# Moving four modulations out of the norms of a two-block transformer kernel

## The chip, the cores and the metric

The kernel runs on one core of a Trainium2 chip. Its time is in device microseconds. The engines are TensorE (PE), VectorE (DVE), ScalarE (ACT), GpSimd (POOL) and SyncE (SP, which issues the DMAs here). All of them run at once; each takes its own instructions in order.

## The reference

256 tokens of width 1,024 pass through two layers of a first block and then two layers of a second block, all in fp32. The change concerns the first block alone:

```python
c_act = jax.nn.silu(c)
for l in range(DEPTH):                                   # 2
    mod = c_act @ w_ada[l] + b_ada[l]
    sh1, sc1, g1, sh2, sc2, g2 = jnp.split(mod, 6, axis=-1)
    h = rmsnorm(x, norm_mix_g[l]) * (1.0 + sc1) + sh1
    z = h @ w_in[l]                                      # four mixers: swa, mla, nsa, moba
    x = x + g1 * (concat(mixers(z)) @ w_out[l])
    h = rmsnorm(x, norm_mlp_g[l]) * (1.0 + sc2) + sh2
    x = x + g2 * (square(relu(h @ w_up[l])) @ w_down[l])
x = rmsnorm(x, final_norm_g)
```

`mod` is six vectors of 1,024 for each layer, one row of `c_act` against a 1,024 x 6,144 matrix. In this text (l, s) is modulation s of layer l: s = 0 is sh1, 1 sc1, 2 g1, 3 sh2, 4 sc2 and 5 g2. Each needs 4 MB of `w_ada`.

## The kernel before

Tokens stand along the free axis and features on the 128 partitions, so x is a tile of 8 chunks of 128 x 256. A weight matrix product is done as three products of fp32r parts: each weight piece of 128 x 1,024 is copied to a high part `wh` on ScalarE (line 299) and its rest `wl` is subtracted on VectorE (line 301); activations are split likewise (`ah`, `al`). One `gemm` is 256 output features: 48 products of 128 x 128 against 128 x 256.

All weights pass through one list in the order of use, `e.stream(...)` (lines 513 to 535). `next_w` (line 304) takes the next piece, splits up to four pieces ahead (NS) and fetches up to eight more (NW); the fetches are one queue on SP. Modulation weights and the compression weights are used whole, without a split.

The program is a list of small steps: `e.add(tag, fn)` appends one, `e.need(tag)` runs steps until none with that tag is left, `e.fill(n)` runs n of them. A planner then orders each engine's instructions by priority and by its own estimate of when their inputs are ready; `high_priority(offset=...)` moves a group forward (200 for the norms, 100 for the splits), and `issue_after(ins)` keeps an instruction behind another one on the same engine.

The stages of the first block are: norm, mixers (line 725), norm, wide products (`w_up` and `w_down` in 16 groups, lines 1066 to 1082), the same again for layer 1, then the last norm. A norm squares x on ScalarE (`square`, line 449), adds the squares on VectorE (`fold`, line 432, `fold_sum`, 441), sums over the partitions on TensorE (`token_sum`, 406, tile `st`), takes the power on GpSimd (`rsqrt`, 401, tile `rsy`), spreads it over the partitions on TensorE (`spread`, 411, tile `bc`), and then scales the 8 chunks: VectorE (603, `nt`), ScalarE (604, `ah`), VectorE (605, `al`).

A modulation is computed in one of two ways. `ada_step` (line 551) takes one of four pairs of weight pieces on TensorE: eight products of 128 x 32 against 128 x 256, which the trace shows as 16 records; four steps are 64 records. `ada_pool` (574) multiplies and adds on GpSimd, one pair at a time, beside the wide products, and `ada_rows` (587) then sums over the partitions with four products on TensorE. Both end in `ada_end` (564): a copy, four small products that turn the row into columns (tile `adat`), and an addition of the bias.

Before, the modulations stand as follows. (0,0) and (0,1) are computed at the start. (0,2), (0,3) and (0,4) are spread over the mixers of layer 0 on TensorE (`ad_early`, `ad_mix`). (1,0), (1,1) and (1,5) are done on GpSimd beside the wide products (`ad_mlp`). (0,5) and (1,4) stand on TensorE in the norm ahead of the wide products of their layer (`ad_norm`, lines 1010 to 1012), and (1,2) and (1,3) in the norm between the layers (`ad_next`, lines 1083 and 997).

Of the kernel before, what the change touches and what calls it, by code (L numbers as in the profile page):

```python
# [13 lines left out]
ALU = mybir.AluOpType  # L14
PSUM = bass.MemoryType.PSUM

P = 128
S = 256
D = 1024
KC = D // P  # L20
DEPTH = 2
# [199 lines left out]
v3 = lambda tl, a: tl.rearrange("p (a b) -> p a b", a=a)  # L221
# [3 lines left out]
class Emit:  # L225
# [157 lines left out]
    def tok_gemm(self, tag, key, act, evac):  # L383
# [14 lines left out]
        for n in range(4):  # L398
            self.add(tag, lambda n=n: piece(n))

    def rsqrt(self, pool, v, cols):
        y = self.t(pool, [P, cols], "rsy", bufs=2)
        self.nc.gpsimd.tensor_tensor(y, v, self.mhalf[:, 0:cols], ALU.pow)  # L403
        return y
# [48 lines left out]

    def rms_wide(self, pool, x, eps):
        box = []
        with self.tc.high_priority(offset=NORM_FIRST):
            for j in range(4):
                self.square(pool, box, flat(x[:, 2 * j : 2 * j + 2, :]))
            return self.rstd(pool, self.fold_sum(box), D, eps)

# [33 lines left out]
def block1(e, ctx, mem0):  # L494
    nc, tc, d = e.nc, e.tc, e.d
    pool = lambda name: ctx.enter_context(tc.tile_pool(name=name, bufs=1))
    cp, zp, ap_ = pool("c1"), pool("z1"), pool("a1")
# [5 lines left out]
    ada = lambda l, s: [("w_ada", l, s, n) for n in range(4)] if l < DEPTH else []  # L503
    zorder = (0, 1, 2, 3, 5, 4, 6, 7, 8)


    ad_early = lambda l: ada(l, 2) if l == 0 else []
    ad_mix = lambda l: ada(l, 3) + ada(l, 4) if l == 0 else []
    ad_norm = lambda l: ada(l,5) if l == 0 else ada(l,4)
    ad_mlp = lambda l: [(1,0),(1,1)] if l == 0 else [(1,5)]  # L510
    ad_next = lambda l: ada(l+1,2)+ada(l+1,3)
    mlp_keys = lambda l: {1 + 6 * i + n: [("w_ada", *p, n)] for i, p in enumerate(ad_mlp(l)) for n in range(4)}
    MEM = 5
    a0 = ada(0, 0) + ada(0, 1)
    start = [[], a0[0:2], a0[2:4], a0[4:6], []]
# [6 lines left out]
    for l in range(DEPTH):  # L522
        W = lambda i: ("w_in1", l, zorder[i])
        ea, am = ad_early(l), ad_mix(l)
        e.stream(*([] if l else [W(0)]), W(1), W(2), *ea[0:2], ("cmp_k1", l), W(3), *ea[2:3], ("cmp_v1", l), W(4), *ea[3:4], W(5))
        e.stream(W(6), *am[0:2], ("w_out1", l, 0), *am[2:3], W(7), ("w_out1", l, 1), *am[3:4], W(8), *am[4:])
        e.stream(("w_out1", l, 2), ("w_out1", l, 3), ("w_up", l, 0), *ad_norm(l))
        nxt = mlp_keys(l)
        for g in range(16):
            if g >= 1:  # L530
                e.stream(("w_up", l, g))
                e.stream(("w_down", l, g - 1))
            e.stream(*nxt.get(g, []))
        e.stream(("w_down", l, 15), *([("w_in1", l + 1, zorder[0])] if l + 1 < DEPTH else []), *ad_next(l))
    e.stream(*MEM_KEYS(0)[MEM:])
# [4 lines left out]
    ca = e.t(cp, [P, KC], "ca")  # L540
# [7 lines left out]

    boxes = {}

# [9 lines left out]
    def blocks(ps, c, w, start, stop):  # L560
        for j in range(4):
            e.mm(ps[32 * j : 32 * j + 32, 0:S], c, w[:, j * S : (j + 1) * S], start, stop)
# [11 lines left out]
    def ada_pool(l, s, n):  # L574
# [4 lines left out]
        for i in range(2):  # L579
# [4 lines left out]
            if not first:  # L584
                nc.gpsimd.tensor_tensor(rows, rows, dst, ALU.add)

    def ada_rows(l, s):
        ps = e.gbank("ada")
        blocks(ps, ones32, boxes[l, s], True, True)
        ada_end(l, s, ps)  # L590

    def ada_add(tag, keys):
        for key in keys:
            e.add(tag, lambda key=key: (ada_pool if tag == "mlp" else ada_step)(*key[1:]))

    def norm_stats(src):
        return e.rms_wide(ap_, src, 1e-6)

# [22 lines left out]
    x = v3(e.unit("x"), KC)  # L621
    nc.sync.dma_start(x, d["xT"])
    e.need("start2")
    bc0 = norm_stats(x)
# [365 lines left out]
    for l in range(DEPTH):  # L990
# [4 lines left out]
        if l:  # L995
            bc0 = norm_stats(x)
            e.need("next")
        norm_apply(x, bc0, A1, mod[:, 0:8], ah, al)
# [10 lines left out]
        ah, al = v3(e.unit("ah", F32R), KC), v3(e.unit("al", F32R), KC)  # L1009
        ada_add("norm", ad_norm(l))  # L1010
        bc0 = norm_stats(x)
        e.need("norm")
        A2 = e.t(ap_, [P, KC], "A2")
# [51 lines left out]

        parts, box, last = {}, [], {}
        steps = mlp_keys(l)
        for g in range(17):
            if l + 1 == DEPTH and g == 1:
                e.add("mlp", late_mem)  # L1070
            if g < 16:
                e.gemm("mlp", [("w_up", l, g)], lambda i: (ah, al), ev_up(g))
            if 1 <= g < 16:
                for c in range(2):
                    e.add("mlp", lambda g=g, c=c: down_piece(g - 1, c))
            if g == 16:
                e.add("mlp", lambda: down_last(15))
            ada_add("mlp", steps.get(g, []))
            for i, p in enumerate(ad_mlp(l)):
                if g == 6 * i + 8:  # L1080
                    e.add("mlp", lambda p=p: ada_rows(*p))
        e.need("mlp")
        ada_add("next", ad_next(l))
        for k in range(KC):
            nc.vector.scalar_tensor_tensor(x[:, k, :], acc[k // 2][:, (k % 2) * S : (k % 2 + 1) * S], mod[:, 40 + k : 41 + k], x[:, k, :], ALU.mult, ALU.add)

    for k in range(MEM, 6):
        mem_gemm(e, 0, k, box[0], mk0, mv0)
    bc = norm_stats(x)
    e.need("mem")  # L1090
# [637 lines left out]
```

## Time and profile before

| | us |
|---|---|
| median of 3 runs (lowest, highest) | 1832.56 (1829.42, 1836.35) |
| the profiled execution's own time | 1832.16 |
| its span, first to last instruction | 1830.3 |
| TensorE busy in the span | 1789.1 |
| VectorE, ScalarE, GpSimd busy | 1333.6, 1016.8, 359.1 |
| moved by DMA | 346.82 MB, 189 GB/s on average |

A product's duration in the profile includes its way through the array, so the next one starts before it has ended: a wide product is listed with 0.28 us, and 40 us hold 339 of them. The granted clock is the share of TensorE's full clock, 2.4 GHz; its other level is half of that. "[1.10 <-POOL rsy]" behind a row says that the engine stood idle for 1.10 us before it and that the instruction which ended the wait was GpSimd's power.

### The profile page before, as it was taken

The numbers are of one execution on the slowest core, as the hardware profiler recorded it, in microseconds if no ns is written. First come the engines' busy times: TensorE is split into PE (matmuls) and PEld (weight loads), VectorE is DVE, ScalarE is ACT, GpSimd is POOL, SyncE is SP. The second block draws the span as 40 slices with busy tenths as digits, with TensorE's granted clock in tenths as the row PEclk, the third lists the DMA queues.
The fourth block names the chain that finished last, engine by engine and source line by source line (L and its number), as shares of the span: only waits on it lengthen the run. The fifth ranks groups of instructions, "written<-read, shape, count | busy, mean of one in ns | idle before, by whom it ended". The sixth has DMA issues, their size and how long they took to land.

```text
span 1830.3 us, 36255 instructions
## 1 busy us (share of the span) xinstructions
PE 1789.1 (98%) x14344; PEld 1674.3 (91%) x14344; DVE 1333.6 (73%) x2209; ACT 1016.8 (56%) x1882; POOL 359.1 (20%) x291
## 2 busy tenths in 40 slices
PE   7999999999998999999999999999999999999998
PEld 6778799987888999998999999999999999999997
DVE  4575775756778655798897997576788797997566
ACT  4444444434555444567777575454556777675552
POOL 0000281800007200002444202200001444202200
PEclk9999999999998999999999999999999999999999
DMA  9873876758348655553444644465554445544451
GB/s 335 308 249 138 310 259 199 256 197 306 115 140 299 226 183 185 165 175 121 162 162 151 202 155 144 168 208 173 194 176 133 148 160 162 184 164 165 154 181 67
DMA packets 98219, 346.82 MB, mean 189 GB/s; under 512 B 12288, under 2 KB 13440, under 8 KB 97792
## 3 DMA queue, kind: packets, MB, share of 16 engines
q1 hardware_dynamic: 98048, 344.50, 55.5%
q8 instruction: 112, 1.84, 0.4%
q14 instruction: 59, 0.48, 0.1%
HBM read 339.01 MB, written 1.05 MB: 186 GB/s over the span
## 4 chain that ended last, share of the span: by engine, by line
PE 89%; DVE 4%; DMA 3%; ACT 3%; issue 1%; SPq 0%; POOLq 0%; DVEq 0%; POOL 0%; ACTq 0%
PE g L337 67%; PE acc L337 10%; PE yps L337 2%; DVE wl L301 1%; ACT wh L299 1%; PE ada L337 1%; PE o L337 1%; PE ds L337 1%; PE sc L337 1%; DMA w<-w_in 1%; PE do L337 1%; DMA w<-w_ada 1%; ACT sb L683 1%; PE xo L337 1%; DMA w<-w_up 1%
## 5 line engine op out<-in xcount | busy, mean ns | idle before, releaser
L301 DVE TENSOR_TENSOR wl<-w,wh 128x1024 fp32r<-128x1024 f32 x518 | 660.8, 1279 | 342.8 <-ACT wh L299 341.1
L299 ACT CAST wh<-w 128x1024 fp32r<-128x1024 f32 x518 | 540.5, 1047 | 494.9 <-PE g L337 328.8
L337 PE MATMUL g<-xh,wh 128*128 128x256 f32 x1664 | 478.2, 288 | 0.3
L337 PE MATMUL g<-xl,wh 128*128 128x256 f32 x1664 | 472.6, 284 | 0.0
L337 PE MATMUL g<-xh,wl 128*128 128x256 f32 x1664 | 471.8, 284 | 0.0
L337 PEld LDWEIGHTS g<-xh,wh 128*128 128x128 f32 x1664 | 319.8, 192 | 12.6 <-issue 6.2
L337 PEld LDWEIGHTS g<-xl,wh 128*128 128x128 f32 x1664 | 319.8, 192 | 0.9 <-issue 0.7
L337 PEld LDWEIGHTS g<-xh,wl 128*128 128x128 f32 x1664 | 319.9, 192 | 0.0
L337 PE MATMUL g<-ah,wh 128*128 128x256 f32 x736 | 211.5, 289 | 5.9 <-ACT ah L604 5.4
L337 PE MATMUL g<-ah,wl 128*128 128x256 f32 x736 | 210.6, 287 | 0.5 <-DVE wl L301 0.5
L337 PE MATMUL g<-al,wh 128*128 128x256 f32 x736 | 210.5, 287 | 0.5 <-DVE al L605 0.5
L403 POOL TENSOR_TENSOR rsy<-rv,mhalf 128x2 f32<-128x2 f32 (+1 forms) x14 | 14.5, 1038 | 936.8 <-DVE rv L420 830.1
L337 PE MATMUL acc<-pt,wh 128*128 128x256 f32 x1024 | 182.9, 280 | 0.0
L1505 POOL PARTITION_BROADCAST E<-rows x64 | 98.0, 1592 | 386.7 <-PE tw L1209 190.9
L1504 ACT ACTIVATE E<-E,ltok 128x128 f32<-128x128 f32 x384 | 124.3, 394 | 60.2 <-POOL E L1505 56.8
L337 PEld LDWEIGHTS acc<-pt,wh 128*128 128x128 f32 x1024 | 156.8, 188 | 0.5 <-issue 0.4
L337 PEld LDWEIGHTS g<-ah,wh 128*128 128x128 f32 x736 | 142.7, 195 | 9.8 <-ACT ah L604 6.4
L337 PEld LDWEIGHTS g<-al,wh 128*128 128x128 f32 x736 | 142.8, 194 | 2.7 <-DVE al L605 1.4
L337 PEld LDWEIGHTS g<-ah,wl 128*128 128x128 f32 x736 | 142.8, 194 | 1.2 <-DVE wl L301 0.7
L337 PE MATMUL acc<-pt,wl 128*128 128x256 f32 x512 | 142.3, 279 | 0.0
L583 POOL TENSOR_SCALAR sb<-w,ca 128x1024 f32<-128x1024 f32 x24 | 90.0, 3751 | 59.9 <-PE ada L337 32.8
L337 PEld LDWEIGHTS acc<-pt,wl 128*128 128x128 f32 x512 | 96.2, 188 | 0.0
(384 smaller groups left out, 3404.8 us busy)
## 6 DMA issues: line engine op xcount, KB each, us to landing
w<-w_ada SPq DMA_DIRECT2D x96, 512.0 KB
w<-w_up SPq DMA_DIRECT2D x64, 512.0 KB
w<-w_down SPq DMA_DIRECT2D x64, 512.0 KB
w<-w_br SPq DMA_DIRECT2D x64, 512.0 KB
w<-w_gl SPq DMA_DIRECT2D x48, 512.0 KB
w<-w_in SPq DMA_DIRECT2D x36, 512.0 KB
w<-w_xs SPq DMA_DIRECT2D x32, 512.0 KB
w<-w_z SPq DMA_DIRECT2D x32, 512.0 KB
```

The costliest lines, as they stand in the source:

```text
L299: nc.scalar.copy(wh, w)
L301: nc.vector.tensor_tensor(wl, w, wh.bitcast(F32), ALU.subtract)
L337: self.last_mm = self.nc.tensor.matmul(o, l, r, start=start, stop=stop)
L403: self.nc.gpsimd.tensor_tensor(y, v, self.mhalf[:, 0:cols], ALU.pow)
L583: nc.gpsimd.tensor_scalar(dst, w, ca[:, 2 * n + i : 2 * n + i + 1], None, ALU.mult)
L683: nc.scalar.activation(self.src(i), self.src(i), AF.Exp, bias=nmx[:, i : i + 1], scale=scale, accum_out=den[:, i : i + 1])
L1504: ex = lambda o, s, r: nc.scalar.activation(o, o, AF.Exp, bias=bias[:, s, r : r + 1])
L1505: nc.gpsimd.partition_broadcast(E, state["rows"][32 * (h % 4) : 32 * (h % 4) + 1, :])
```

## The change

- (0,5) and (1,2) are computed on VectorE beside the wide products of layer 0. `ada_fetch` loads a pair of weight pieces (1 MB) into one of the 11 shared buffers of 128 x 2,048, two groups ahead; `ada_vec` multiplies it by the entries of c and adds, two instructions over 1,024 columns for each pair, ordered behind the last subtraction of the group before (`last["dve"]`). `ada_rows` is put six steps further down the list.
- (1,3) and (1,4) move from the norms into the mixers of layer 1, on TensorE, at the places that (0,2) and (0,3) have in layer 0.
- `ad_norm` and `ad_next` go. In the norms stand products of the identity with itself whose output nobody reads, `warm`: `ahead` of the sums, `between` sums and spread, and `behind` the spread. The numbers are 8, 4, 5 in the norms ahead of the wide products, 12, 4, 5 between the layers, and 0, 5, 5 in the last norm.

```diff
+    def warm(self, o, n):
+        with self.tc.issue_after(self.last_mm.ins):
+            for _ in range(n):
+                self.nc.tensor.matmul(o, self.ident, self.ident, start=True, stop=True)
...
-    def rms_wide(self, pool, x, eps):
+    def rms_wide(self, pool, x, eps, ahead=0, between=0, behind=0):
         box = []
+        if ahead:
+            self.warm(self.gbank("warm")[:, 0:P], ahead)
         with self.tc.high_priority(offset=NORM_FIRST):
             for j in range(4):
                 self.square(pool, box, flat(x[:, 2 * j : 2 * j + 2, :]))
-            return self.rstd(pool, self.fold_sum(box), D, eps)
+            st = self.fold_sum(box)
+            if between:
+                self.warm(self.bank("warm")[:, 0:P], between)
+            bc = self.rstd(pool, st, D, eps)
+            if behind:
+                self.warm(self.bank("warm")[:, 0:P], behind)
+        return bc
...
-    ad_early = lambda l: ada(l, 2) if l == 0 else []
-    ad_mix = lambda l: ada(l, 3) + ada(l, 4) if l == 0 else []
-    ad_norm = lambda l: ada(l,5) if l == 0 else ada(l,4)
-    ad_next = lambda l: ada(l+1,2)+ada(l+1,3)
+    ad_early = lambda l: ada(0, 2) if l == 0 else ada(1, 3)
+    ad_mix = lambda l: ada(0, 3) + ada(0, 4) if l == 0 else ada(1, 4)
+    ad_vec = lambda l: ada(0, 5) + ada(1, 2) if l == 0 else []
...
+    def ada_fetch(l, s, n):
+        boxes["w", l, s, n] = e.unit("adaw")
+        nc.sync.dma_start(boxes["w", l, s, n], d["w_ada"][l, s, n])
+
+    def ada_vec(l, s, n):
+        if n == 0:
+            if "rows" not in boxes:
+                boxes["rows"] = v3(e.unit("rows"), 2)
+            boxes[l, s] = boxes["rows"][:, 0 if l == 0 else 1, :]
+        rows, w = boxes[l, s], v3(boxes.pop(("w", l, s, n)), 2)
+        for i in range(2):
+            c = ca[:, 2 * n + i : 2 * n + i + 1]
+            with tc.issue_after(last["dve"].ins):
+                if n == 0 and i == 0:
+                    nc.vector.tensor_scalar(rows, w[:, i, :], c, None, ALU.mult)
+                else:
+                    nc.vector.scalar_tensor_tensor(rows, w[:, i, :], c, rows, ALU.mult, ALU.add)
+        if n == 3:
+            e.q.insert(min(6, len(e.q)), ("mlp", lambda: ada_rows(l, s)))
...
-            bc0 = norm_stats(x)
-            e.need("next")
+            bc0 = norm_stats(x, 12, 4, 5)
...
-        ada_add("norm", ad_norm(l))
-        bc0 = norm_stats(x)
-        e.need("norm")
+        bc0 = norm_stats(x, 8, 4, 5)
...
+        at = lambda j: 3 + 3 * j // 2
         for g in range(17):
+            for j, key in enumerate(vec):
+                if at(j) == g + 2:
+                    e.add("mlp", lambda key=key: ada_fetch(*key[1:]))
...
+            for j, key in enumerate(vec):
+                if at(j) == g:
+                    e.add("mlp", lambda key=key: ada_vec(*key[1:]))
...
-        ada_add("next", ad_next(l))
...
-    bc = norm_stats(x)
+    bc = norm_stats(x, 0, 5, 5)
```

## Rows read from the trace of the kernel before

**Rows 1.** Stretches: length, busy us per engine (instructions), granted clock, DMA share, GB/s

```profile
67.90:205.40 137.50, 136.18 (x1157) 111.23 (x1155) 87.98 (x267) 60.35 (x149) 2.31 (x2) 1.00 0.63 224
205.40:223.60 18.20, 14.18 (x125) 11.89 (x125) 12.86 (x27) 8.21 (x14) 6.33 (x3) 0.81 0.86 314
423.00:546.20 123.20, 118.80 (x956) 103.30 (x954) 88.39 (x260) 60.87 (x147) 2.57 (x2) 0.99 0.49 169
546.20:565.40 19.20, 14.12 (x125) 12.28 (x125) 13.95 (x26) 8.31 (x14) 8.38 (x4) 0.73 0.90 346
484.00:494.00 10.00, 10.00 (x67) 7.91 (x65) 4.67 (x23) 5.36 (x20) 0.00 (x0) 0.84 0.16 54
757.70:763.70 6.00, 6.00 (x28) 6.00 (x29) 5.17 (x14) 2.75 (x7) 0.00 (x0) 0.50 0.34 98
320.00:360.00 40.00, 40.00 (x339) 40.00 (x338) 29.99 (x22) 19.07 (x22) 38.91 (x13) 1.00 0.77 258
```

**Rows 2.** Timeline of TensorE, layer 0's second norm: start, us, instruction, xcount, [idle <-releaser]

```profile
205.42 3.66 PE L337 MATMUL ada<-w,ca 128*32 128x256 f32 x64
...
210.72 0.71 PE L337 MATMUL bc<-pack,rsy 128*128 128x128 f32 x4 [1.10 <-POOL rsy L403]
...
223.54 0.28 PE L337 MATMUL g<-al,wh 128*128 128x256 f32 x1
```

**Rows 3.** Timeline of VectorE, the same norm

```profile
207.89 0.42 DVE L444 TENSOR_TENSOR fold<-fold 128x256 f32<-128x256 f32 x1
...
211.22 1.23 DVE L301 TENSOR_TENSOR wl<-w,wh 128x1024 fp32r<-128x1024 f32 x1 [1.33 <-ACT wh L299]
...
220.76 1.67 DVE L605 SCALAR_TENSOR_TENSOR al<-nt,mod,ah 128x256 fp32r<-128x256 f32 x2 [0.18 <-ACT ah L604]
```

**Rows 4.** Timeline of TensorE, layer 1's first norm

```profile
409.26 0.61 PE L337 MATMUL st<-ones,fold 128*128 128x1 f32 x4
...
422.87 0.28 PE L337 MATMUL g<-ah,wl 128*128 128x256 f32 x1
...
424.28 0.38 PE L337 MATMUL g<-ah,wl 128*128 128x256 f32 x1 [0.45 <-DVE wl L301]
```

**Rows 5.** Timeline of VectorE, layer 1's first norm

```profile
406.33 0.43 DVE L444 TENSOR_TENSOR fold<-fold 128x256 f32<-128x256 f32 x1
...
411.74 0.87 DVE L603 SCALAR_TENSOR_TENSOR nt<-x,A,bc 128x256 f32<-128x256 f32 x2 [1.61 <-PE bc L337]
...
418.36 0.89 DVE L605 SCALAR_TENSOR_TENSOR al<-nt,mod,ah 128x256 fp32r<-128x256 f32 x2 [0.19 <-ACT ah L604]
```

**Rows 6.** Timeline of VectorE, layer 1's second norm

```profile
548.71 0.43 DVE L444 TENSOR_TENSOR fold<-fold 128x256 f32<-128x256 f32 x1
...
563.78 3.06 DVE L605 SCALAR_TENSOR_TENSOR al<-nt,mod,ah 128x256 fp32r<-128x256 f32 x2 [0.18 <-ACT ah L604]
```

**Rows 7.** Timeline of TensorE, layer 1's second norm: its 48th wide product

```profile
565.35 0.28 PE L337 MATMUL g<-ah,wh 128*128 128x256 f32 x1
```

**Rows 8.** Timeline of TensorE, layer 1's mixers: the longest hole

```profile
482.36 1.08 PE L337 MATMUL o<-pt,z 128*64 128x256 f32 x4 [2.12 <-ACT pt L710]
```

**Rows 9.** Timeline of TensorE, layer 0's wide products: the end of a GpSimd modulation

```profile
384.78 0.64 PE L337 MATMUL ada<-sb,ones 128*32 128x256 f32 x8
...
388.55 0.50 PE L337 MATMUL adat<-pack,pt 128*128 128x4 f32 x4
```

**Rows 10.** Groups by line, 320 to 360 us: busy us, mean ns of one, idle before

```profile
L301 DVE TENSOR_TENSOR wl<-w,wh 128x1024 fp32r<-128x1024 f32 x14 | 24.7, 1769 | 10.1 <-ACT wh L299 10.1
L583 POOL TENSOR_SCALAR sb<-w,ca 128x1024 f32<-128x1024 f32 x6 | 23.3, 3875 | 0.6
L585 POOL TENSOR_TENSOR sb<-sb,sb 128x1024 f32<-128x1024 f32 x7 | 18.2, 2607 | 0.6
```

**Rows 11.** Line 1239, VectorE over 1,024 columns: ns min/median/max

```profile
L1239 DVE SCALAR_TENSOR_TENSOR r<-r,mv,gb x2: 1274/1275/1276, 1819.2 to 1824.3; 128x1024 f32<-128x1024 f32 x2
```

**Rows 12.** Timeline of GpSimd, layer 0's second norm

```profile
217.96 5.92 POOL L583 TENSOR_SCALAR sb<-w,ca 128x1024 f32<-128x1024 f32 x2 [7.30 <-DMA w<-w_ada]
```

More of the change, by code (lines that the diff above doesn't have):

```diff
@@ L504, in block1 @@
     zorder = (0, 1, 2, 3, 5, 4, 6, 7, 8)
-    ad_early = lambda l: ada(l, 2) if l == 0 else []
-    ad_mix = lambda l: ada(l, 3) + ada(l, 4) if l == 0 else []
-    ad_norm = lambda l: ada(l,5) if l == 0 else ada(l,4)
-    ad_mlp = lambda l: [(1,0),(1,1)] if l == 0 else [(1,5)]
-    ad_next = lambda l: ada(l+1,2)+ada(l+1,3)
+    ad_early = lambda l: ada(0, 2) if l == 0 else ada(1, 3)
+    ad_mix = lambda l: ada(0, 3) + ada(0, 4) if l == 0 else ada(1, 4)
+    ad_mlp = lambda l: [(1, 0), (1, 1)] if l == 0 else [(1, 5)]
+    ad_vec = lambda l: ada(0, 5) + ada(1, 2) if l == 0 else []
     mlp_keys = lambda l: {1 + 6 * i + n: [("w_ada", *p, n)] for i, p in enumerate(ad_mlp(l)) for n in range(4)}
@@ L526, in block1 @@
         e.stream(W(6), *am[0:2], ("w_out1", l, 0), *am[2:3], W(7), ("w_out1", l, 1), *am[3:4], W(8), *am[4:])
-        e.stream(("w_out1", l, 2), ("w_out1", l, 3), ("w_up", l, 0), *ad_norm(l))
+        e.stream(("w_out1", l, 2), ("w_out1", l, 3), ("w_up", l, 0))
         nxt = mlp_keys(l)
@@ L533, in block1 @@
             e.stream(*nxt.get(g, []))
-        e.stream(("w_down", l, 15), *([("w_in1", l + 1, zorder[0])] if l + 1 < DEPTH else []), *ad_next(l))
+        e.stream(("w_down", l, 15), *([("w_in1", l + 1, zorder[0])] if l + 1 < DEPTH else []))
     e.stream(*MEM_KEYS(0)[MEM:])
@@ L547, in block1 @@
     mods = [e.t(cp, [P, 48], f"mod{l}") for l in range(DEPTH)]
-    boxes = {}
+    boxes, last = {}, {}
     def ada_step(l, s, n):
@@ L594, in ada_add, with norm_stats @@
             e.add(tag, lambda key=key: (ada_pool if tag == "mlp" else ada_step)(*key[1:]))
-    def norm_stats(src):
-        return e.rms_wide(ap_, src, 1e-6)
+    def norm_stats(src, *idle):
+        return e.rms_wide(ap_, src, 1e-6, *idle)
     def norm_apply(src, bc, A, sh, ah, al):
@@ L1064, in late_mem @@
                 box.append(load_mem(e))
-        parts, box, last = {}, [], {}
+        parts, box, vec = {}, [], ad_vec(l)
+        at = lambda j: 3 + 3 * j // 2
         steps = mlp_keys(l)
```

## The prediction

> **What bounds the kernel now.** I read the stretches first, then the timelines of the norms, and the mixers last. In the wide products TensorE has no idle time (40.00 of 40 us, 0.118 us a product), so a piece of TensorE work put there costs its full length and nothing else in that stage is worth anything [rows 1]. What can be won lies in the four norms between the stages, where TensorE waits for a chain (squares on ScalarE, folds on VectorE, the sums on TensorE, a power on GpSimd, the spread on TensorE, then eight rounds of scaling). I call them A (layer 0, ahead of its wide products), B (layer 1, ahead of its mixers), C (layer 1, ahead of its wide products) and D (the last). Around A and C the mean granted clock is 0.81 and 0.73, and the first 6.0 us of products behind D run at 0.50, that is at 1.2 of 2.4 GHz [rows 1]. In front of the sums the modulation's products stand on TensorE: in A they run from 205.42 to 209.08, while the folds were done at 208.31 [rows 2, 3].
>
> The mixers are full too: 118.80 of 123.20 us in layer 1. Layer 0 has the same products plus three modulations and takes 137.50 us for the same part, from behind the first 48 products to the last product of `w_out1` [rows 1]. This pair of rows prices what the change moves there.
>
> **The norms.** B shows the chain undisturbed from the sums on: sums at 409.26, scaling from 411.74, the last round ended at 419.25 [rows 4, 5], which is 2.48 + 7.51 = 10.0 us; with 0.6 us for the last five of the first 48 products, 10.6 us from the sums to the 48th. In the changed kernel the sums can start 0.06 us behind the last fold.
> - A: folds done 207.89 + 0.42, so 208.37 + 10.6 = 218.9 against 223.54 [rows 2, 3]: 4.6 us. I take 0.8 off since GpSimd lengthens a pair of subtractions there (1.67 against 0.89 us), as it will again, and 0.8 for part of one weight split of 1.23 us that falls into the chain now, at 211.22, and may again [rows 3, 5]. Left: 3.0.
> - B: folds done 406.76, so 417.4 against 422.87: 5.5 us, less 0.4 for a third of a split [rows 3 to 5]. Left: 5.1. The sixteen transfers of 512 KB for two modulations no longer stand ahead of the next weights, whose split is waited for at 424.28 [rows 4].
> - C: folds done 549.14, so 559.8 against 565.35: 5.6 us [rows 6, 7]. GpSimd stretched the last pair by 2.17 us here (3.06 against 0.89), so I take 1.8 off. Left: 3.8.
> - D: no modulation goes. 28 products in 6.0 us at half clock would need 28 x 0.118 = 3.3 us at the full one, 2.7 less [rows 1]; the first of them wait for the scaling anyway, so 2.2, less 0.3 because five idle products ahead of the spread overrun their gap. Left: 1.9.
>
> The idle products: no row shows one. The nearest is the spread, two fp32 products of 128 columns in 0.71 us, 0.36 us each with the tail [rows 2]; from the other side, two records of half the columns of a wide product (0.118 us) make 0.12. I take 0.25, between the two: twelve make 3.0, eight 2.0, four 1.0, five 1.25. In B they start when the accumulation ends at about 403.7 and end at 406.7, before the sums; in A they end at 207.4. Between sums and spread there are 1.1 us free [rows 2]. So they cost nothing on the path; at 0.36 us twelve would hold the sums of B by 1.2 us. That they keep the clock up is judged by B, where TensorE was fed through the norm and no slow stretch follows.
>
> **The mixers of layer 1.** (1,3) and (1,4) go in, at the places that (0,2) and (0,3) have in layer 0. By the two stretches, three modulations cost 137.50 - 123.20 = 14.3 us, 4.8 each, though 64 records in one run take 3.66 and the four turning products 0.50 [rows 1, 2, 9]: split up among other products they take longer than in one run. Two cost 9.5. From it goes what stands at the head of this stretch today, a turning and a wait for a split, 0.50 + 0.45, say 1.0 us [rows 4, 9]. I take +8.5. The upper bound is 9.5 (nothing returned). The lower: 2 x (3.66 + 0.50) = 8.3, less the hole of 2.12 us that they could fill, less the slow clock at 484 to 494 (0.84 over 10 us, so 3.2 us at half rate, 1.6 lost) and less 1.0: +3.6 [rows 1, 8]. Their DMAs, sixteen of 512 KB, enter a stretch whose DMA share is 0.49; with three modulations it is 0.63 in layer 0 [rows 1], so I cost them at nothing.
>
> **The wide products of layer 0.** (0,5) and (1,2) become sixteen VectorE instructions over 1,024 columns at 1.27 us [rows 11], 20.4 us, behind the last subtraction of a group; TensorE gets twice eight products (0.64 us at most) and four turnings (0.50): 2.3 us at most, 1.9 without the tails under which the next product starts [rows 9]. I take +1.9. VectorE is idle in 10.0 of 40 us beside a GpSimd modulation [rows 10], so ten instructions' worth in 46 us has about 11.5 us to go into; what overruns is taken by the three pieces of split weights ahead (24 products each, 2.8 us). The eight fetches of 1 MB add 8.4 MB to 180 us, 47 GB/s on 258, below the 346 GB/s that C shows [rows 1]. Each is issued two groups (some 23 us) ahead of its use. A new instruction waits for its fetch; behind it on VectorE stand the weight splits, and TensorE waits for those. Cost 0 with this cover; without it the price is that of the second rival.
>
> **Sum.** -3.0 - 5.1 - 3.8 - 1.9 + 8.5 + 1.9 = -3.4 us. The profiled execution took 1832.16 us, 1.86 more than its span and 0.40 below the median of the runs. 1832.16 - 3.4 = 1828.8.
>
> **Rivals.**
> - The mixers swallow the two modulations and the norms give all: -4.6 - 5.5 - 5.6 - 2.2 + 3.6 + 1.9 = -12.4, 1819.8 us. For it speaks the hole of 2.12 us right where (0,3) fills the same place in layer 0; against it, that layer 0 is 14.3 us longer with the same fill.
> - VectorE and GpSimd block each other in the wide products. Beside GpSimd's products a split takes 1.77 us on average against 1.23 elsewhere [rows 3, 10]. If each new instruction had to sit out one GpSimd addition (2.61 us), eight of them in the second modulation's 46 us would cost 8 x (1.27 + 2.61) = 31.0 against 11.5 of idle time. The splits run about 6.3 us ahead (three pieces, 8.6, less a copy and a split, 2.3), so TensorE would stand for 31.0 - 11.5 - 6.3 = 13.2 us: 1828.8 + 13.2 = 1842.0, slower than before. It decides from a mean wait of about 1 us per instruction on. Against it: today's mean wait is 0.54 us. The Trainium skill, "SBUF — State Buffer", section "Who interferes with whom", states that a VectorE instruction with two SBUF inputs contends with a GpSimd instruction that reads SBUF, and that the later one fully blocks. By that rule the new instructions are of the kind that blocks, and the sum would be this rival's; the trace shows the blocking, at less than a third of the price.
> - GpSimd starts its first product ahead of the power in A and C. Today it waits until 217.96 for weights that stood behind (0,5) [rows 12]; with these gone they come earlier, and one 3.88 us product [rows 10] in front of the power would delay each of the two norms by up to that: 1828.8 + 2 x 3.9 = 1836.6. Against it: the power has the higher priority when the order is made.
> - The idle products do not hold the clock. The gains by start time stay, those of the clock go: 1.9 in D, about 1 each in A and C: 1832.7.
>
> **How the numbers follow.** Forecast 0.50, with its own range 1824 to 1833; the mixers swallow it 0.22; blocking 0.09; GpSimd first 0.09; clock not held 0.10. The range 1819 to 1838 leaves out the blocking and a little of each tail. 0.5% is 9.2 us, about what a measurement here tells from no change. Faster by more (below 1823): most of the first rival and the forecast's tail, 0.24. Slower by more (above 1841): blocking and a tail, 0.10. Within: 0.66.
>
> **What would show it.** Right: from the folds' end to the 48th product about 11 to 12 us in A, B and C, with a clock near 1 in all four norms; the stretch of layer 1's mixers some 8 us longer, with 128 modulation records in it; the wide products of layer 0 about 2 us longer with no idle TensorE. Wrong: mixers longer by under 5 us (then faster), idle TensorE waiting for a split in 320 to 365 us (then slower), a GpSimd product in front of the power, or a stretch at 0.5 behind a norm.

## The result: slower, and the profile after

The changed kernel takes 1850.24 us (median of 4 runs, 1846.53 to 1851.33) against 1833.82 us (median of 4, 1829.42 to 1836.35): ratio 1.0089, 95% interval [1.0064, 1.0114]. The forecast was 1828.8 with a range to 1838, so it was wrong on the side as well. The profiled execution took 1851.33 us, 19.2 more than that of before; the stages below account for 19.1 of this. Each ends with the start of a product that both traces have: a norm runs from the last product of the stage ahead to the 48th product behind it. The traced execution of held_ad below was a disturbed one (8352 us), so no stage of it is read, and all ratios compare undisturbed executions.

| stage | before, us | after, us | difference | forecast |
|---|---|---|---|---|
| start | 67.90 | 69.61 | +1.7 | 0 |
| mixers, layer 0 | 137.31 | 137.66 | +0.4 | 0 |
| norm A | 18.33 | 22.28 | +3.9 | -3.0 |
| wide products, layer 0 | 180.03 | 181.98 | +1.9 | +1.9 |
| norm B | 19.31 | 16.08 | -3.2 | -5.1 |
| mixers, layer 1 | 123.16 | 135.63 | +12.5 | +8.5 |
| norm C | 19.31 | 17.98 | -1.3 | -3.8 |
| wide products, layer 1 | 178.37 | 180.05 | +1.7 | 0 |
| D and the rest | 1079.00 | 1080.55 | +1.5 | -1.9 |
| sum | | | +19.1 | -3.4 |

The stretches of the changed kernel (length, busy us of PE, PEld, DVE, ACT, POOL with instructions, granted clock, DMA share, GB/s):

```profile
207.30:229.60 22.30, 13.95 (x93) 13.38 (x92) 17.82 (x23) 5.37 (x10) 17.24 (x8) 0.85 0.65 237
320.00:360.00 40.00, 40.00 (x345) 39.28 (x345) 34.94 (x26) 17.60 (x21) 36.80 (x11) 1.00 0.67 216
427.60:563.30 135.70, 132.62 (x1089) 109.29 (x1088) 89.40 (x259) 60.82 (x149) 9.70 (x5) 1.00 0.58 190
775.20:781.20 6.00, 6.00 (x50) 5.92 (x49) 5.21 (x14) 2.82 (x7) 0.00 (x0) 1.00 0.28 98
```

The four stretches are norm A, 40 us of layer 0's wide products, layer 1's mixers and the first products behind D. Against [rows 1]: GpSimd works 17.24 us inside A where it worked 6.33. TensorE has no idle time in the wide products although sixteen VectorE instructions were added to the stage; VectorE's idle time there fell from 10.0 to 5.1 us of 40. The mixers of layer 1 hold 133 more products, and the clock behind D is 1.00.

Norm A in the timelines (start, us, instruction, xcount, [idle <-releaser]), TensorE first, then VectorE, then GpSimd:

```profile
207.39 1.95 PE L405 MATMUL warm<-pack 128*128 128x128 f32 x16
215.16 0.98 PE L337 MATMUL st<-ones,fold 128*128 128x1 f32 x4 [5.82 <-DVE fold L450]
...
229.55 0.28 PE L337 MATMUL g<-ah,wh 128*128 128x256 f32 x1
```

```profile
205.69 1.22 DVE L301 TENSOR_TENSOR wl<-w,wh 128x1024 fp32r<-128x1024 f32 x1
...
207.61 1.49 DVE L444 TENSOR_TENSOR fold<-pt,pt 128x512 f32<-128x512 f32 x1
...
209.80 1.21 DVE L301 TENSOR_TENSOR wl<-w,wh 128x1024 fp32r<-128x1024 f32 x1
210.93 3.62 DVE L444 TENSOR_TENSOR fold<-fold,pt 128x512 f32<-128x512 f32 x2
214.59 0.42 DVE L450 TENSOR_TENSOR fold<-fold 128x256 f32<-128x256 f32 x1
...
220.01 3.02 DVE L640 SCALAR_TENSOR_TENSOR al<-nt,mod,ah 128x256 fp32r<-128x256 f32 x2 [0.19 <-ACT ah L639]
...
225.85 3.00 DVE L640 SCALAR_TENSOR_TENSOR al<-nt,mod,ah 128x256 fp32r<-128x256 f32 x2 [0.19 <-ACT ah L639]
```

```profile
204.60 5.68 POOL L597 TENSOR_SCALAR sb<-w,ca 128x1024 f32<-128x1024 f32 x2 [119.93 <-DVE x L1039]
210.36 2.84 POOL L599 TENSOR_TENSOR sb<-sb,sb 128x1024 f32<-128x1024 f32 x1
216.49 0.72 POOL L409 TENSOR_TENSOR rsy<-rv,mhalf 128x2 f32<-128x2 f32 x1 [3.28 <-DVE rv L426]
...
220.13 2.61 POOL L599 TENSOR_TENSOR sb<-sb,sb 128x1024 f32<-128x1024 f32 x1
...
225.82 2.35 POOL L599 TENSOR_TENSOR sb<-sb,sb 128x1024 f32<-128x1024 f32 x1
```

GpSimd's products of (1,0) start at 204.60, ahead of the norm; before, their weights stood behind (0,5) and they began at 217.96 [rows 12]. Three of its additions fall on the folds and on two pairs of subtractions: two folds take 3.62 us, two pairs 3.02 and 3.00 against 0.89 undisturbed [rows 5]. One weight split stands just ahead of the folds and one among them; before, they came behind them [rows 3]. The folds end at 215.01, 7.7 us behind the last product of the mixers, where they took 3.1; from there to the 48th product it is 14.5 us, where the prediction had 10.6. GpSimd's power itself was not late: GpSimd stood idle for 3.28 us before it, waiting for VectorE. The idle products were over at 209.34, and a stretch at half clock runs from 214.0 to 220.8.

The same thing ends the mixers of layer 1: a VectorE split, a GpSimd addition of (1,5), and the wait of TensorE that follows (VectorE, GpSimd, TensorE, the same kernel):

```profile
555.84 3.22 DVE L301 TENSOR_TENSOR wl<-w,wh 128x1024 fp32r<-128x1024 f32 x1
```

```profile
555.58 2.40 POOL L599 TENSOR_TENSOR sb<-sb,sb 128x1024 f32<-128x1024 f32 x1
```

```profile
559.91 0.39 PE L337 MATMUL g<-oh,wh 128*128 128x256 f32 x1 [1.10 <-DVE x L1039]
```

The split starts 0.26 us into the addition and ends 1.08 us behind its end (557.98): it seems to have lain still and then run in nearly its usual 1.22 us.

### The profile page after: what moved, and what is told of

Same layout as the page of the kernel before. It is cut to its first block, busy times and chain, and to the rows that moved or that the text cites. A ratio compares the mean times of both kernels' runs of the same rounds, so it can differ in the third digit from the quotient of the medians.

```text
span 1849.5 us, 36289 instructions
## 1 busy us (share of the span) xinstructions
PE 1802.6 (97%) x14362; PEld 1687.3 (91%) x14362; DVE 1359.2 (73%) x2225; ACT 1016.6 (55%) x1882; POOL 354.6 (19%) x291
## 4 chain that ended last, share of the span: by engine, by line
PE 88%; DVE 5%; ACT 3%; DMA 2%; issue 1%; SPq 0%; POOLq 0%; DVEq 0%; POOL 0%; ACTq 0%
PE g L337 65%; PE acc L337 10%; DVE wl L301 2%; PE yps L337 1%; PE ada L337 1%; PE o L337 1%; ACT wh L299 1%; PE sc L337 1%; PE ds L337 1%; PE do L337 1%; PE xs L337 1%; PE xo L337 1%; ACT sb L718 1%; PE tp L743 1%; PE warm L405 1%
## 5 line engine op out<-in xcount | busy, mean ns | idle before, releaser
L597 POOL TENSOR_SCALAR sb<-w,ca 128x1024 f32<-128x1024 f32 x24 | 84.7, 3529 | 319.6 <-DVE x L1039 124.0
```

Of the source, the lines that this page charges most:

```text
L597: nc.gpsimd.tensor_scalar(dst, w, ca[:, 2 * n + i : 2 * n + i + 1], None, ALU.mult)
```

## The experiments

My theory after the comparison: the modulations that left A and C let GpSimd's products and the splits run into the norms, which eats the gain; and the mixers cost more per modulation than I took. Rival: the idle products, or the new order of the work, delay the chain. Each account below opens with the kernel's ratio to the kernel before on the same chip, with a 95% interval; "before, with" names the kernel that is edited, and "..." in a diff stands for lines left out. Stage lengths (us) come from one trace of each kernel. Layer 0's mixers, which all but none_l0 and gp_mixers leave as they were, took 136.1 to 139.8 us in these traces and 142.3 in held_runs, so a difference of 2 us or so in one stage of two traces proves little by itself.

| kernel | A | wide 0 | B | mixers 1 | C | wide 1 |
|---|---|---|---|---|---|---|
| mix_only | 16.67 | 180.03 | 18.74 | 135.81 | 20.33 | 178.37 |
| vec_only | 19.81 | 182.11 | 19.57 | 123.42 | 20.35 | 178.39 |
| after_no_idle | 20.87 | 182.13 | 17.31 | 133.43 | 20.49 | 178.37 |
| after_gp_held | 16.44 | 186.23 | 15.71 | 133.91 | 16.00 | 181.50 |
| splits_held | 14.21 | 187.15 | 13.93 | 136.24 | 16.09 | 181.41 |
| both_held | 16.15 | 184.38 | 14.99 | 134.45 | 14.07 | 180.83 |
| held_norms | 13.89 | 184.36 | 18.56 | 124.87 | 19.60 | 181.12 |
| c_held | 18.49 | 181.60 | 20.95 | 129.05 | 15.29 | 184.04 |

**mix_only.** Before, with:

```diff
-    ad_early = lambda l: ada(l, 2) if l == 0 else []
+    ad_early = lambda l: ada(0, 2) if l == 0 else ada(1, 3)
-    ad_mix = lambda l: ada(l, 3) + ada(l, 4) if l == 0 else []
+    ad_mix = lambda l: ada(0, 3) + ada(0, 4) if l == 0 else ada(1, 4)
...
```

> The kernel before with one part of the change alone: (1,3) and (1,4) move from the norms B and C into layer 1's mixers; (0,5) stays in A, (1,2) in B, no idle products. Theory 1 (the two modulations cost about 12 us wherever the rest of the change stands): the mixers' stretch of layer 1 grows from 123.2 to about 135.5 us, B gives 2 to 3 us for one run of 64 products less, C gives 0 to 1; the time is 8 to 10 us above before, ratio 1.0045 to 1.0055. Rival (the mixers grow by the forecast 8.5 us, and the rest of the +12.5 comes from other parts of the change, as GpSimd's products that run into the end of the mixers): stretch 131 to 132 us, ratio 1.002 to 1.003.

1.0077 [1.0063, 1.0091], mixers 135.81: the +12.5 us belong to these two modulations alone. The norms gave less than expected, B 0.6 us and C nothing, and the ratio is above the expected 1.0045 to 1.0055.

**vec_only.** The changed kernel with `norm_stats(x)` (no idle products), (1,3) back in B, (1,4) back in C.

> The kernel before with one part alone: (0,5) and (1,2) go to VectorE in layer 0's wide products; (1,3) stays in B, (1,4) in C, no idle products. Theory 1 (with (0,5) gone the weights reach GpSimd and the splits before norm A ends, and these stretch its folds and subtractions): wide products of layer 0 +2.0 us, A 21 to 23 us instead of 18.3, B 2 to 3 us shorter; in sum +1.5 to +4, ratio 1.001 to 1.002. Rival (A lost because the idle products stand in it): A 15 to 16 us, in sum -3 to -4, ratio 0.998.

1.0038 [1.0023, 1.0053], above the expected 1.002; B gave nothing where 2 to 3 us were expected. A took 19.81 with no idle products and nothing moved into the mixers, so A's loss needs neither, and the idle products are out as its cause.

**after_no_idle.** The changed kernel with `norm_stats(x)` in all norms.

> The changed kernel without its idle products. Theory 1 (they only feed the clock and cost no time on the path): the slow stretch behind D comes back (+2.2 us), A stays at 21 to 23 us; ratio to before 1.009 to 1.011. Rival (the idle products delay the sums or shift the order of the work, and are what makes the change slow): A falls to 16 us, ratio to before 1.004 to 1.006.

1.009 [1.0074, 1.0105]: without the idle products the time is the same as with them. A stays at 20.87, but C takes 20.49 us against 17.98. There GpSimd put a product and this addition ahead of its power, whose input VectorE had ready at 567.90:

```profile
568.03 2.34 POOL L599 TENSOR_TENSOR sb<-sb,sb 128x1024 f32<-128x1024 f32 x1
570.33 0.73 POOL L409 TENSOR_TENSOR rsy<-rv,mhalf 128x2 f32<-128x2 f32 x1
```

And no slow stretch came back behind D:

```profile
772.90:778.90 6.00, 6.00 (x49) 5.96 (x50) 5.20 (x14) 2.79 (x7) 0.00 (x0) 1.00 0.28 98
```

So the full clock behind D is not theirs: it is 1.00 without them too, as in mix_only and vec_only.

**after_gp_held.** The changed kernel, and GpSimd reads its factors from a copy made behind the last subtraction:

```diff
+            with tc.issue_after(end.ins):
+                nc.vector.tensor_copy(boxes["cg"], ca)
...
-            nc.gpsimd.tensor_scalar(dst, w, ca[...], None, ALU.mult)
+            nc.gpsimd.tensor_scalar(dst, w, boxes["cg"][...], None, ALU.mult)
```

> The changed kernel, with GpSimd's products of a layer's wide stage held until the norm's last subtraction (they read their factors from a copy that VectorE makes behind it; 128x8, two copies added). Theory 1a (GpSimd's products blocking VectorE are what A and C lost): folds of A end 3 to 4 us earlier, no subtraction above 1 us, A 18 to 19.5 us instead of 22.3; C 2 us shorter, the hole of 1.26 us at the end of layer 1's mixers gone; ratio to before 1.004 to 1.006. Rival 1b (the weight splits that stand among the folds are what A lost): A keeps 21 us or more, ratio to before 1.008 or more.

1.0053 [1.004, 1.0067], as expected. A fell to 16.44, further than the expected 18 to 19.5, and C to 16.00, 2 us as expected. The wide products of layer 0 grew by 4.2 us, which no theory had: TensorE, in the window behind A,

```profile
230.93 0.39 PE L337 MATMUL g<-ah,wh 128*128 128x256 f32 x1 [0.42 <-ACT wh L299]
...
232.69 0.58 PE L337 MATMUL g<-ah,wl 128*128 128x256 f32 x1 [1.26 <-DVE wl L301]
```

waits for a weight piece whose copy ScalarE began late:

```profile
229.83 1.05 ACT L299 CAST wh<-w 128x1024 fp32r<-128x1024 f32 x1 [3.60 <-PE g L337]
```

Start to start the two holes cost 2.0 us, and a stretch of 3.4 us at half clock follows (232.7 to 236.1).

**splits_held.** The changed kernel, in which the splits of the next stage's weights, from the second matrix piece on, wait for the norm's last square and last fold:

```diff
+            for ins in self.gate or ():
+                cx.enter_context(self.tc.issue_after(ins))
...
-            if not self._whole(ent) and split < NS:
+            if not self._whole(ent) and split < NS and not past:
```

> The changed kernel, with the weight splits of the second and later wide keys held behind the norm's last fold (GpSimd is not held). Theory 1a (GpSimd's two-input additions cost A and C most, the splits little): A 20.5 to 22 us against 22.3, since the folds still stand beside the additions; ratio to before 1.007 to 1.010. Rival 1b (the splits cost as much as GpSimd): A 18 us, ratio 1.005.

1.0051 [1.0034, 1.0068], A 14.21: the rival 1b was nearer, and A fell further than it had. The two causes are not a sum. With the splits out of the way the folds were done (212.57) before the first addition began (215.46), so holding either one frees most of A.

**both_held.** Both edits.

> The changed kernel with both held: GpSimd's products behind the norm's last subtraction, the splits behind its last fold. If the two together are all that A and C lost: A and C 15 to 15.8 us (16.4 and 16.0 with GpSimd held alone), and no TensorE hole of 2.0 us in front of the fifth weight piece of the wide products; ratio to before 1.002 to 1.004, the rest being layer 1's mixers. If another thing stands in the norms: A stays at 16.4 or more.

1.0019 [1.0009, 1.0029], at the lower end of what was expected. VectorE in A of both_held, then the kernel's stretches for A, B, layer 1's mixers and C:

```profile
209.44 0.42 DVE L458 TENSOR_TENSOR fold<-fold 128x256 f32<-128x256 f32 x1
209.79 1.22 DVE L305 TENSOR_TENSOR wl<-w,wh 128x1024 fp32r<-128x1024 f32 x1
...
215.13 0.89 DVE L650 SCALAR_TENSOR_TENSOR al<-nt,mod,ah 128x256 fp32r<-128x256 f32 x2 [0.18 <-ACT ah L649]
```

```profile
206.80:223.00 16.20, 13.80 (x93) 13.45 (x92) 11.09 (x23) 6.34 (x11) 1.61 (x1) 0.79 0.54 196
...
407.30:422.30 15.00, 13.46 (x101) 13.11 (x100) 11.13 (x23) 6.28 (x11) 1.64 (x1) 0.89 0.52 173
422.30:556.80 134.50, 132.93 (x1089) 110.37 (x1088) 87.25 (x263) 60.94 (x150) 1.40 (x2) 0.99 0.54 182
556.80:570.90 14.10, 11.49 (x92) 10.74 (x92) 11.26 (x23) 6.36 (x11) 1.61 (x1) 1.00 0.55 172
```

The folds end at 209.86, 3.1 us behind the last product, as the prediction had it; C is 14.07, a gain of 5.2 against the ideal 5.6 [rows 6, 7]. The hole in the wide products shrank only to 1.5 us. A keeps 16.15, since 6.8 us of it ran at half clock; with a full clock (splits_held, held_norms) it is 14. What remains is the mixers and the price of holding in the wide products.

**mix_runs** (mix_only with each modulation in one run of 64 products) and **held_runs** (the same in both_held):

```diff
...
-        ada_add("E", ea[3:4])
+        ada_add("E", ea[3:4] if l == 0 else ea)
...
-        ada_add("o0", am[2:3])
+        ada_add("o0", am[2:3] if l == 0 else am)
```

> mix_only with each of the two modulations in one run of 64 products (behind the products of E, and behind those of o0) in place of four pieces each. Theory 2a (the two cost 12.5 us and not 8.3 because each piece is woven into other products and pays at every change of kind): layer 1's mixers 130 to 132 us, 4 below mix_only, ratio to before 1.0050 to 1.0060. Rival 2b (TensorE loses it to waits and to the clock, not to the weaving): 135 us or more, ratio 1.007 to 1.009.

> both_held with the two modulations of layer 1's mixers in one run of 64 products each, as in mix_runs. Theory (the gains of mix_runs and of both_held add): mixers 131 to 132.5 us, the rest as both_held; ratio to before 0.999 to 1.001. Rival (the run takes the splits' or the chain's time here too): mixers 134 or more, ratio 1.002.

mix_runs: 1.0071 [1.0056, 1.0087] with mixers of 132.53, 3.3 us less than woven and near 2a's 130 to 132; held_runs: 1.0044 [1.0031, 1.0058] with 137.02, 2.6 more than woven. In time the runs gain nothing in either, as 2b had it. But held_runs' traced execution is the longest of its five, and layer 0's mixers, which it leaves alone, are 4.1 us longer in it too, so the 2.6 us are not the runs' alone. What the modulations' own products take of TensorE did fall (tile `ada` in the mixers of mix_only, then of mix_runs; the second and third figure are busy us of PE and PEld):

```profile
422.40:558.30 135.90, 10.60 (x128) 4.04 (x128) 0.72 (x2) 1.00 0.56 195
```

```profile
424.20:556.80 132.60, 7.74 (x128) 3.75 (x128) 0.74 (x2) 0.99 0.54 195
```

So weaving has a price, 2.9 us for the two in these traces, but undoing it did not shorten the kernel.

**one_13, three_l1, none_l0.** Edits of the same two lines of before, for what stands in the mixers: in layer 1 (1,3) alone; in layer 1 (1,2), (1,3) and (1,4); and in layer 0 nothing, where (0,2), (0,3) and (0,4) are left out and a constant stands in their place.

> The kernel before with (1,3) alone moved into layer 1's mixers; (1,4) stays in C, (1,2) in B. By 6.2 us each (theory 3a: every modulation has the same price) the mixers take 129.4 us and 3 to 4 us more where a slow stretch falls into them or not; if the first is dear and the next cheap (3b) 131 to 133. Ratio to before 1.001 to 1.003.

> The kernel before with (1,2), (1,3) and (1,4) in layer 1's mixers, at the very places that (0,2), (0,3) and (0,4) have in layer 0. If the layers are alike (3b: the price of a modulation depends on what is beside it): 137 to 139 us, as in layer 0, so the third costs some 2 us. If every one costs 6.2 us (3a): 141 to 143. Ratio to before 1.006 to 1.009.

> The kernel before with layer 0's (0,2), (0,3) and (0,4) left out (their columns of the table hold a constant 0.5), so that layer 0's mixers run without any. If the layers are alike without modulations: 121 to 123.5 us, 14 to 16 below before. If layer 0's base is shorter (3c): 117 to 119. Ratio to before 0.990 to 0.993.

1.0031 [1.0019, 1.0043], 1.0069 [1.0054, 1.0084], 0.9941 [0.9924, 0.9958]. The mixers of mix_only, one_13, three_l1 and (layer 0) none_l0:

```profile
422.40:558.30 135.90, 132.85 (x1089) 109.14 (x1087) 88.95 (x258) 60.25 (x148) 11.41 (x5) 1.00 0.56 195
```

```profile
425.00:554.70 129.70, 125.56 (x1021) 106.63 (x1019) 85.47 (x258) 59.37 (x146) 4.18 (x2) 0.97 0.47 163
```

```profile
418.90:556.30 137.40, 136.18 (x1157) 111.52 (x1155) 87.03 (x261) 60.04 (x149) 4.30 (x4) 1.00 0.59 211
```

```profile
68.50:192.00 123.50, 119.44 (x952) 103.76 (x951) 86.31 (x261) 59.02 (x146) 1.50 (x2) 0.97 0.41 141
```

Without a modulation and with three the layers are alike: 123.2 and 123.5 us, 137.3 and 137.3, so 3c falls. By these traces one costs 6.5, two 12.6 and three 14.1, the third 1.5. 3a was right for one (129.4) and wrong for three (141 to 143); 3b was right for three and wrong for one (131 to 133). The own products of one and three modulations (tile `ada`, one_13 and three_l1):

```profile
425.00:554.70 129.70, 4.69 (x64) 1.88 (x64) 0.35 (x1) 0.97 0.47 163
```

```profile
418.90:556.30 137.40, 15.08 (x192) 6.04 (x192) 1.11 (x3) 1.00 0.59 211
```

With mix_only's 10.60 that is 4.7, 10.6 and 15.1 us: the third takes its share of TensorE like the others. It is the rest of the stage that differs, 125.0, 125.3 and 122.3 us; TensorE stood idle there for 4.1, 3.1 and 1.2 us, and the granted clock was 0.97, 1.00 and 1.00. Two modulations took 133.4 to 136.2 us in the six kernels that weave them in, so the 1.5 us for the third are no firmer than that.

**ad_14, held_ad, c_held.** (1,4) alone in one run at the end of the mixers, `ada_add("ad", am[4:] if l == 0 else am)`: in before, in both_held with (1,3) back in B, and in before with C alone held.

> The kernel before with (1,4) alone moved, in one run at the end of layer 1's mixers, the place that the third modulation has in layer 0; (1,3) stays in B. Theory 4a (the price is that of the place): mixers 124.5 to 126 us, ratio to before 1.000 to 1.001. Rival 4b (the first modulation is dear wherever it stands): 129 us or more, as in one_13, ratio 1.002 to 1.004.

> both_held with (1,3) back in norm B (one run of 64, no idle products ahead) and (1,4) in one run at the end of layer 1's mixers. By the stages measured so far: mixers 125 (4a) or 129 (4b), B 18.6, C 14.1, the rest as both_held; that is 1831 to 1833 or 1835 to 1837, ratio 0.998 to 1.000 or 1.001 to 1.002.

> The kernel before with (1,4) in one run at the end of layer 1's mixers, and in C alone GpSimd and the splits held and idle products added; (0,5) stays in A, (1,2) and (1,3) in B, nothing goes to VectorE. By the stages so far: mixers +1.5 to 3 (4a), C -5, wide products of layer 1 +2.5, the rest as before: -1 to +0.5, ratio 0.9995 to 1.0005; by 4b +3, ratio 1.002.

ad_14: 1.0066 [1.0053, 1.0079] with mixers of 131.17; held_ad: 1.0028 [1.0019, 1.0038]; c_held: 1.0042 [1.003, 1.0054] with mixers of 129.05. All three ratios are above what either theory had. A single modulation at the place of the third cost 8.0 us in one trace and 5.9 in the other, not 1.5, so place alone does not explain it: 4a falls. In ad_14 norm C grew as well, to 23.68 us. In c_held norm C is 4.0 us shorter than in before, and the wide products behind it are 5.7 longer.

**held_norms.** both_held with (1,3) back in B, (1,4) back in C.

> both_held with (1,3) back in norm B and (1,4) back in C, in one run of 64 products each (no idle products ahead of these two norms); only (0,5) and (1,2) are out of the norms, on VectorE. Theory (11.3 us of both_held's mixers against before are the two moved modulations, and a run of 64 in a norm costs it 3 to 5 us): layer 1's mixers 123.5 us, B 18 to 19.5, C 17.5 to 19.5; 3 us below both_held, ratio to before 0.999 to 1.001. Rival (with GpSimd and the splits held a run in the norm is covered by the chain): B and C 15 to 16, ratio 0.995 to 0.998.

1.0023 [1.0014, 1.0032]: the mixers fall to 124.87, B and C rise to 18.56 and 19.60 (theory, not rival); the ratio is a little above the expected 1.001. Against both_held that is 9.6 us less in the mixers and 9.1 more in the two norms: the two modulations cost about the same in either place.

**all_wide.** both_held with all of it in layer 0's wide products:

```diff
...
+    ad_mlp = lambda l: [(1, 0), (1, 1), (1, 3)] if l == 0 else [(1, 5)]
+    ad_vec = lambda l: ada(0, 5) + ada(1, 2) + ada(1, 4) if l == 0 else []
...
```

> both_held with (1,3) as a third GpSimd modulation in layer 0's wide products (one every five groups in place of every six) and (1,4) as a third one on VectorE there; none in layer 1's mixers. Theory: the mixers go back to 123.5 us, the wide products take 183 to 186 us, A, B and C 15 to 16 each; in sum 3 to 7 below before, ratio 0.996 to 0.998. Rival (twelve more VectorE instructions and 46 us more of GpSimd block each other, and the splits come late): wide products of 190 us or more with TensorE idle, ratio 1.001 or more.

1.0118 [1.0103, 1.0133]: the rival. The wide products of layer 0 take 199.7 us, with TensorE idle for 8.9 of them, and behind them stands a B of 26.8, where TensorE waits for the third modulation on GpSimd:

```profile
426.76 1.08 PE L345 MATMUL ada<-sb,ones 128*32 128x256 f32 x8 [5.49 <-POOL sb L609]
```

**gp_mixers, gp_mixers_l1.** both_held with (l,3) and (l,4) on GpSimd in the mixers, rows and products in two spare tiles:

```diff
...
+                nc.gpsimd.tensor_scalar(ptmp[:, i, :], w, c, None, ALU.mult)
+                nc.gpsimd.tensor_tensor(rows, rows, ptmp[:, i, :], ALU.add)
...
```

> both_held with (0,3), (0,4), (1,3), (1,4) on GpSimd in their layer's mixers, where GpSimd is all but idle, in place of 64 TensorE products each; TensorE keeps 8 products and 4 turnings for each. Theory (a modulation costs the mixers 5 to 6 us only because it takes TensorE's time, and VectorE has room there, 88 of 123 us): layer 0's mixers 128 to 131 us instead of 138, layer 1's 125 to 128 instead of 134.5; ratio to before 0.990 to 0.995. Rival (some thirty GpSimd additions a layer hold up VectorE's splits and the chain of the attention, and TensorE waits): mixers no shorter than in both_held, ratio 1.002 or more.

> both_held with (1,3) and (1,4) alone on GpSimd, in layer 1's mixers. Theory: those 125 to 128 us instead of 134.5, the rest as in both_held; ratio to before 0.996 to 0.999. Rival (additions hold up VectorE): 133 us or more, ratio 1.001 or more.

1.0388 [1.0373, 1.0403] and 1.0197 [1.018, 1.0214]: the theory failed outright, with mixers of 169.9 us in layer 0 and 158.8 in layer 1 (159.2 in gp_mixers_l1). VectorE, GpSimd and TensorE of gp_mixers, layer 0:

```profile
133.00 3.18 DVE L305 TENSOR_TENSOR wl<-w,wh 128x1024 fp32r<-128x1024 f32 x1 [0.36 <-ACT wh L303]
136.10 2.31 DVE L752 TENSOR_TENSOR den<-den,se 128x8 f32<-128x8 f32 x1
...
144.47 6.59 DVE L758 TENSOR_SCALAR sb<-sb,den 128x128 f32<-128x128 f32 x8
```

```profile
132.70 5.69 POOL L644 TENSOR_TENSOR prow<-prow,ptmp 128x1024 f32<-128x1024 f32 x2
...
144.14 4.81 POOL L644 TENSOR_TENSOR prow<-prow,ptmp 128x1024 f32<-128x1024 f32 x2
```

```profile
151.81 1.51 PE L345 MATMUL o<-pt,z 128*64 128x256 f32 x3 [7.31 <-DVE pt L773]
```

An instruction over eight columns takes 2.31 us beside the additions, and TensorE, which needs the last link of the attention's chain (`pt`), waits 7.31 us.

## Why the prediction was wrong

- **Norm A is the step that failed most** (7.0 of 22.5 us): "folds done 207.89 + 0.42, so 208.37 + 10.6 = 218.9". It took the folds' end from a trace in which (0,5) stood ahead of the next weights, and removed (0,5). Counted from the last product of the mixers the folds ended 4.6 us later than that, and the chain behind them took 3.9 us more than the 10.6, of which the prediction had allowed 1.6. [rows 12] showed the consequence: GpSimd waits for weights. I used it in the third rival, but asked only whether GpSimd would delay its own power; in the changed kernel it delayed VectorE's folds and subtractions (the power was late in C of after_no_idle, by 2.4 us). after_gp_held, splits_held and both_held show this: 16.4, 14.2 and 16.2 us against 22.3. The sizes were right once these were held: 4.1 to 4.4 us gained at full clock against an ideal of 4.6.
- **C** failed in the same way: 1.3 gained where 3.8 was forecast, 5.2 in both_held. So did **B** in part: splits at 412.64 among its folds; 3.2 against 5.1, 4.3 in both_held. Holding has a price of its own: both_held's wide products take 184.4 and 180.8 us against 182.1 and 178.4 in after_no_idle. The same kind of hole makes 1.5 of the +1.7 us in the changed kernel's own wide products of layer 1, which the prediction had at 0; TensorE there:

```profile
587.67 0.38 PE L337 MATMUL g<-ah,wh 128*128 128x256 f32 x1 [0.42 <-ACT wh L299]
...
588.93 0.39 PE L337 MATMUL g<-ah,wl 128*128 128x256 f32 x1 [0.76 <-DVE wl L301]
```

- **Layer 1's mixers**, the term mis-sized by 4.0 us: "three modulations cost 14.3 us for the same part, 4.8 each". The total was right (14.1), but two cost 12.6 and not 9.5. The bound of 9.5 was none, because it assumed a straight line and that the rest of the stage stays as it is. The own products of the two take 10.6 us in mix_only, and where I took 1.0 us off the rest of the stage, it is 2.1 us longer than without modulations (125.3 against 123.2); with three it is 0.9 shorter. Why the rest moves so is open: weaving and place, the two explanations tried, do not account for it, and single traces of one program differ by as much.
- **The first rival** (the mixers swallow them) is refuted by mix_only. **The second** (blocking in the wide products) is refuted for two VectorE modulations: no idle TensorE, +1.95 us against a forecast 1.9. With three each on GpSimd and VectorE (all_wide) the wide products were 15 us longer than in both_held and TensorE waited in them, as this rival has it; what part of that is blocking was not separated. The Trainium skill, "SBUF — State Buffer", section "Who interferes with whom", states that a VectorE instruction with two SBUF inputs contends with a GpSimd instruction that reads SBUF, and calls the contention an exclusive lock. Here the trace agrees beside GpSimd's additions (3.62 us for two folds, 3.22 for a split). Beside its one-input products it agrees only in part: the split at 205.69, inside the products of 204.60, took 1.22 us, its usual time, and the fold at 207.61 took 1.49 us against 0.68 in after_gp_held, but ended 1.2 us ahead of them.
- **The idle products**, the fourth rival's subject, cost what was taken at full clock (8 in 1.95 us, 0.24 each, against 0.25) and nearly nothing on the path: in A the four between sums and spread ran at half clock, 2.05 us, and the scaling came 2.70 us behind VectorE's `rv`, against 2.28 in after_no_idle. The slow stretch in A is shorter with them (13.7 us in vec_only and after_no_idle, 0 to 6.8 with them) but not abolished, and D's clock was 1.00 in kernels without them, so that this part of the forecast came true by luck.
- **The rest**: D's products ran at full clock as forecast, and the 192nd product behind D came 2.5 us earlier; but the 400th was only 0.8 us earlier, and block 2, of which no line changed, lost the rest. Its order of work came out differently, with a hole such as this on TensorE of the changed kernel:

```profile
856.97 0.39 PE L337 MATMUL g<-xh,wh 128*128 128x256 f32 x1 [1.31 <-ACT dv L1349]
```

In the changed kernel these holes of over 0.25 us sum to 4.4 us, before to 1.0. c_held speaks for this reading: its TensorE has the same two holes as before, D runs at full clock without idle products there, and "D and the rest" takes 1076.3 us against 1079.0, so D's term was about right and block 2's order lost it. The 1.7 us in the start go with a half-clock stretch (63.8 to 67.2) behind the same instructions. Before has none there, eleven of the kernels above do; the start took 68.5 to 69.6 us with it and 67.5 to 69.0 without, so it need not be all of the 1.7.

No version that computes every modulation beat the kernel before; both_held came nearest at 1.0019.

## What to carry to other kernels

When a step is taken out of a queue, everything behind it comes earlier: list which engine gets work sooner, and what that engine does to the chain that you shorten, before any duration of the old trace is used again. Do not divide a stage's difference by the number of things in it: price one, two and three, in more than one trace each, or say that only the sum is known. And an engine that looks idle is not free where its instructions stop the engine that carries the chain.

## What the runs showed of the hardware

- A GpSimd addition over two SBUF tiles holds up a VectorE instruction with SBUF inputs that starts beside it until the addition ends (a split of 3.22 us against 1.22, eight columns in 2.31 us), while a VectorE instruction with one of its two inputs in PSUM keeps its time. Both stand beside one addition in the changed kernel's wide products (GpSimd, then VectorE; `g` is in PSUM, and the second instruction takes 0.69 us where no addition runs, as at 273.84):

```profile
355.56 2.66 POOL L599 TENSOR_TENSOR sb<-sb,sb 128x1024 f32<-128x1024 f32 x1
```

```profile
355.88 0.68 DVE L1058 TENSOR_TENSOR pt<-pt,g 128x512 f32<-128x512 f32 x1
356.59 2.19 DVE L1059 TENSOR_TENSOR pt<-pt,pt 128x512 fp32r<-128x512 f32 x1
```

- The granted clock can fall in one execution and not in another with the same products ahead: A of both_held ran 6.8 us at 1.2 GHz, A of held_norms none, 16.15 and 13.89 us. The stretch of held_norms:

```profile
206.90:220.80 13.90, 11.48 (x93) 10.73 (x92) 11.12 (x23) 6.28 (x11) 1.61 (x1) 1.00 0.61 206
```
